# One attention layer's PSUM slots, square buffers and norms rearranged in a two-layer trunk kernel

## The chip, the cores and the metric

The kernel runs on one core of a Trainium2 chip. The metric is the device time of one execution in microseconds, the median of several runs; lower is better. The core has five engines that run their own instruction streams and wait for each other by semaphores: PE (matrix multiplication, with PEld for its weight loads), DVE (vector), ACT (scalar, activations), POOL (the general one) and SP (which issues most transfers here). SBUF is the on-chip memory; PSUM holds what PE writes, and DVE and ACT read it from there.

## The reference

Two layers over x of 512 tokens by 1024 features, all in float32. A layer is: half a SwiGLU feed-forward, a mixer, a cross attention to 256 memory tokens, and another half feed-forward. Layer 0's mixer is a stick-breaking attention with a gated mixing branch; layer 1's is the multi-head latent attention that the change touches:

```
def _mla_mixer(h, positions, w_in, q_lora_g, kv_lora_g, w_uq, w_ukv, q_g, k_g, w_out):
    c_q, c_kv, k_r = jnp.split(h @ w_in, [512, 768], axis=-1)
    q  = (_rmsnorm(c_q, q_lora_g) @ w_uq).reshape(b, s, 16, 96)
    kv = (_rmsnorm(c_kv, kv_lora_g) @ w_ukv).reshape(b, s, 16, 128)
    k_nope, v = kv[..., :64], kv[..., 64:]
    k = concatenate([k_nope, broadcast(k_r to 16 heads)])       # 64 + 32
    q = _rmsnorm(q, q_g);  k = _rmsnorm(k, k_g)                 # over each head's 96
    q, k = (_rope on the last 32 of each)
    o = _causal_softmax_attention(q, k, v)                      # 16 heads, scale 96**-0.5
    return o.reshape(b, s, 1024) @ w_out
```

## The kernel before

x stays in SBUF transposed, as eight tiles of 128 features by 512 tokens. Every large product is split into a high and a low part in a format that PE multiplies faster, and runs as three matmuls (`mm3`, L103 to L105: high by high, low by high, high by low). `split` makes the two parts: a high one (L79, on ACT here) and the rest (L83, on DVE).

`mla_attn` treats the 16 heads in four groups of G = 4. `proj_q(g, t)` makes a block of 128 tokens of the queries of a group (12 matmuls into an "A" bank); ACT copies it out (L716) and squares it into a scratch tile (L718, `dg` with a single buffer), and DVE sums the squares (L719). `proj_kv(g, t)` does the same for keys and values (6 matmuls; square L692, sum L693). The last block of a group (t = 3) ends with `norms` (a chain of small DVE instructions, L666 and L111 to L119), the factors `sqr` (L698), and `knorm`, which multiplies the keys by their inverse norms into `ks`: the 64 features of each head (L673) and the 32 shared ones (L674), for the whole group at once, on DVE for group 0 and on POOL otherwise. Then POOL multiplies the group's `qs` by `sqr` (L700).

The attention is one loop over n = 0 to 16. In step n stand, in the order in which PE runs them:

1. `scores(n)`: three "lg" banks; DVE takes row maxima (L827), ACT exponentials with their sums (L831).
2. `weights` of head n - 1: PE turns the exponentials (L845) into "pt" banks, in three units. ACT copies unit 0 out to wT (L850), DVE units 1 and 2 (L852). Units 0 and 1, then fillers, then unit 2.
3. If n is even and two heads are complete: `inverse`. DVE takes reciprocals of the sums of both heads (L859 to L862), PE turns them (L864) into a "pt" bank, and DVE copies them to arT (L867).
4. `turn` for head n + 2: PE turns q (L740, four transposes into a "pt" bank), then k (another "pt" bank). From q's, ACT makes qTh (L79) and DVE qTl (L83); from k's, ACT makes kTh (L747) and DVE kTl (L748).
5. Fillers.
6. If n is even: `spread` (L872, four matmuls with the selector `asel` into the bank in which the inverse was turned; ACT copies it to rbc, L875) and `values` (L887, 16 matmuls of the two heads into "av"; DVE multiplies by rbc, L894, and the product is split into hh and hl, the input of the output projection).
7. Fillers.

The fillers are the projections of later groups, and behind them the first half of the output projection, taken by `take` in the numbers of the table `FILL`; the first 14 steps (`LEAD2`) stand ahead of the loop. PSUM has in this part two "pt" slots, three "lg", one "av" and two "A". A tile of a pool takes the slot that its name frees next, and the first instruction that writes it waits for the last reader of the tile that had the slot before. PE's instructions run in the order written here.

Of the kernel before, what the change touches and what calls it, by code (L numbers as in the profile page):

```python
# [11 lines left out]
ALU = mybir.AluOpType  # L12
AX = mybir.AxisListType

P = 128
D = 1024
S = 512
KT = D // P
NT = S // P
# [7 lines left out]
class Trunk:  # L27
# [626 lines left out]
    def mla_attn(self, p, pl, pp, cT, krr, skr, gqk, neg, tq, o):  # L654
        nc, a = self.nc, self.a
        G = 4
        LEAD2 = 14
        FILL = [(0, 1, 1)] + [(1, 0, 1)] * 8 + [(2, 0, 2)] * 8
# [10 lines left out]

        def knorm(st, y, eng):  # L670
            st["ks"] = ks = self.t(p, [P, NT, G, 96], "ks", bufs=2)
            by = lambda d: y[:, :, :, None].to_broadcast([P, NT, G, d])
            eng.tensor_tensor(out=ks[:, :, :, 0:64], in0=st["kn"], in1=by(64), op=ALU.mult)  # L673
            eng.tensor_tensor(out=ks[:, :, :, 64:96], in0=krr[:, :, None, :].to_broadcast([P, NT, G, 32]), in1=by(32),  # L674
                              op=ALU.mult)

        def proj_kv(st, g, t):

            if t == 0:
                st["wkv"] = self.gran(a["mla_w_ukv"][g], 2, 512, lo="dve" if g < 2 else "pool")  # L680
                st["v"] = self.t(p, [P, NT, G, 64], "vs", bufs=3)
                st["kn"] = self.t(p, [P, NT, G, 64], "kn", bufs=1)
            cs = slice(t * P, (t + 1) * P)
            ps = self.psA()
            wh, wl = st["wkv"]
            for k in range(2):
                self.mm3(ps, (cT[4 + k][0][:, cs], cT[4 + k][1][:, cs]), (wh[:, k, :], wl[:, k, :]), k == 0, k == 1)
            z = ps.rearrange("p (g d) -> p g d", g=G)
            nc.scalar.copy(out=st["kn"][:, t], in_=z[:, :, 0:64])
            nc.scalar.copy(out=st["v"][:, t], in_=z[:, :, 64:128])  # L690
            s2 = self.t(self.sp, [P, NT, P], "dg", bufs=1)[:, :, 0:64]
            nc.scalar.activation(out=s2, in_=z[:, :, 0:64], func=AF.Square)  # L692
            nc.vector.tensor_reduce(out=st["ss"][:, 0, t, :], in_=s2, axis=AX.X, op=ALU.add)  # L693
            if t < NT - 1:
                return
            y = norms(st)
            st["s"] = self.t(p, [P, NT, G], "sqr", bufs=3)
            ts(out=st["s"], in0=y[:, 1], scalar1=96 ** -0.5, scalar2=None, op0=ALU.mult)  # L698
            knorm(st, y[:, 0], nc.vector if g == 0 else nc.gpsimd)
            nc.gpsimd.tensor_tensor(out=st["qs"], in0=st["qs"], in1=st["s"][:, :, :, None].to_broadcast([P, NT, G, 96]),  # L700
                                    op=ALU.mult)

        def proj_q(st, g, t):

            if t == 0:
                st["wq"] = [self.gran(a["mla_w_uq"][2 * g + i], 2, 384, lo="dve" if g < 2 else "pool") for i in range(2)]
                st["qs"] = self.t(p, [P, NT, G, 96], "qs", bufs=2)
                st["ss"] = self.t(p, [P, 2, NT, G], "ssqk", bufs=2)
            cs = slice(t * P, (t + 1) * P)
            qs = st["qs"]  # L710
            ps = self.psA()
            for k in range(4):
                wh, wl = st["wq"][k // 2]
                self.mm3(ps[:, 0:384], (cT[k][0][:, cs], cT[k][1][:, cs]), (wh[:, k % 2, :], wl[:, k % 2, :]),
                         k == 0, k == 3)
            nc.scalar.copy(out=qs[:, t].rearrange("p g d -> p (g d)"), in_=ps[:, 0:384])  # L716
            s1 = self.t(self.sp, [P, NT, P], "dg", bufs=1)[:, :, 0:96]
            nc.scalar.activation(out=s1, in_=ps[:, 0:384].rearrange("p (g d) -> p g d", g=G), func=AF.Square)  # L718
            nc.vector.tensor_reduce(out=st["ss"][:, 1, t, :], in_=s1, axis=AX.X, op=ALU.add)  # L719
            if t < NT - 1:  # L720
                return

            bc = lambda z: z[:, :, None, :].to_broadcast([P, NT, G, 16])
            q1, q2 = qs[:, :, :, 64:80], qs[:, :, :, 80:96]
            w = [self.t(p, [P, NT, G, 16], f"qr{i}", bufs=1) for i in range(3)]
            rt = nc.gpsimd.tensor_tensor
            rt(out=w[0], in0=q1, in1=bc(tq["c1"]), op=ALU.mult)
            rt(out=w[1], in0=q1, in1=bc(tq["s1"]), op=ALU.mult)
            rt(out=w[2], in0=q2, in1=bc(tq["s2"]), op=ALU.mult)
            rt(out=q1, in0=w[0], in1=w[2], op=ALU.subtract)  # L730
            rt(out=w[2], in0=q2, in1=bc(tq["c2"]), op=ALU.mult)
            rt(out=q2, in0=w[1], in1=w[2], op=ALU.add)
# [60 lines left out]
        def take(n, queue=True):  # L793
            for _ in range(n):
                if queue:
                    with self.queued():
                        next(fill, None)
                else:
                    next(fill, None)
# [55 lines left out]
        def inverse(sm):  # L855


            rc = self.t(p, [P, 2 * NT], "arc", bufs=2)
            nc.vector.reciprocal(out=rc, in_=sm.rearrange("p i t -> p (i t)"))  # L859
            r2 = self.t(p, [P, 2, 2 * NT], "ar2", F32R, bufs=2)  # L860
            nc.vector.tensor_copy(out=r2[:, 0], in_=rc)
            tt(out=r2[:, 1], in0=rc, in1=r2[:, 0].bitcast(F32), op=ALU.subtract)  # L862
            ps = self.t(pp, [P, S], "pt", bufs=2)
            nc.tensor.transpose(out=ps[0:16, 0:P], in_=r2.rearrange("p e r -> p (e r)").bitcast(F32),  # L864
                                identity=self.ident)
            rT = self.t(p, [16, P], "arT", F32R, bufs=2)
            nc.vector.tensor_copy(out=rT, in_=ps[0:16, 0:P])  # L867
            rb = self.rbc

            def spread():  # L870
                for t in range(NT):
                    self.pe = nc.tensor.matmul(ps[:, t * P:(t + 1) * P], lhsT=sel[:, t], rhs=rT, start=(t == 0),  # L872
                                               stop=(t == NT - 1), skip_group_check=True)

                nc.scalar.copy(out=rb, in_=ps)  # L875
                return rb
            return spread

        def values(n, wTs, rb):

            g, h = divmod(n, G)
            av = self.t(pp, [P, S], "av", bufs=1)
            for j in range(NT):
                u, c0 = KA[j]
                wd = S - j * P
                for i, wT in enumerate(wTs):
                    self.pe = nc.tensor.matmul(av[i * 64:i * 64 + 64, j * P:], lhsT=gs[g]["v"][:, j, h + i, :],  # L887
                                               rhs=wT[u][:, c0:c0 + wd], start=(j == 0), stop=(j == NT - 1),
                                               skip_group_check=True)
            f = n // 2  # L890
            hi = self.t(self.hp, [P, S], f"hh{f}", F32R)
            lo = self.t(self.hp, [P, S], f"hl{f}", F32R)
            w = self.t(self.sp, [P, S], "sq", bufs=2)
            tt(out=w, in0=av, in1=rb, op=ALU.mult)  # L894
            self.split(hi, lo, w, "act", "dve")
            o.append((hi, lo))

        take(LEAD2, False)
        def ahead(n):

            assert "s" in gs[n // G]
            with self.queued():
                return turn(gs[n // G], n % G)
# [4 lines left out]
        for n in range(17):  # L908
            old = pb
            if n % 2 == 0 and n:  # L910
                sums = self.sums
            if n < 16:
                with self.queued():
                    pb = scores(n, qk.pop(0))
            if old is not None:
                wT = []
                with self.queued():
                    weights(old, wT, (0, 1))
                take(FILL[n][0])
                with self.queued():  # L920
                    weights(old, wT, (2,))
                wTs.append(wT)
            if len(wTs) == 2:
                with self.queued():
                    spread = inverse(sums)
            if n < 14:
                qk.append(ahead(n + 2))
            take(FILL[n][1])
            if len(wTs) == 2:
                with self.queued():  # L930
                    rb = spread()
                with self.queued():
                    values(n - 2, wTs, rb)
                wTs = []
            take(FILL[n][2])


    def xmem(self, l):
# [267 lines left out]
```

## Time and profile before

| what | value |
|---|---|
| median of 3 runs | 2297.13 us |
| range of the runs | 2290.03 to 2308.14 us |
| the profiled execution's own time | 2289.97 us |
| its span, first to last instruction | 2288.3 us |
| its mean granted PE clock | 0.997 |
| busy: PE, PEld, DVE, ACT, POOL | 98%, 82%, 40%, 38%, 45% |
| DMA | 208.68 MB, 91 GB/s on average |

All durations come from the profiled execution. In a row of the timeline the first number is the start in us from the span's start, the second the duration, and the bracket the idle time of the engine ahead of it with the instruction that ended it. In the groups "busy, mean ns" are followed by the group's idle time and what ended most of it. Matmuls are pipelined and their ends are modelled, so two of them in a row may overlap.

### The profile page before, as it was taken

How to read it: one execution, taken by the hardware profiler on the slowest of the kernel's cores; microseconds unless marked ns; L12 is line 12 of the kernel's file. 1: busy time of each engine (PE TensorE's matmuls, PEld its weight loads, DVE VectorE, ACT ScalarE, POOL GpSimd, SP SyncE). 2: the span in 40 equal slices, each digit the busy share in tenths (PEclk: the TensorE clock that was granted, in tenths of full speed). 3: DMA queues.
4: the chain of work that ended last, by engine and by line, in shares of the span. 5: the costliest groups of instructions: out<-in, count | busy, mean ns of one | idle time of the engine just before them, and what ended most of it. 6: DMA issues, size and time to landing. Idle time of an engine off the chain costs nothing. (4 is left out here: it accounts for less than half of the span.)

```text
span 2288.3 us, 29129 instructions
## 1 busy us (share of the span) xinstructions
PE 2250.2 (98%) x11240; PEld 1885.1 (82%) x11240; DVE 907.2 (40%) x1686; ACT 867.4 (38%) x1443; POOL 1018.3 (45%) x824
## 2 busy tenths in 40 slices
PE   8999999999999999999999999998889999999999
PEld 6888888977988888888888888897668988888887
DVE  5211323466745422123422022376558555221220
ACT  4222333366544332223322232356546544322221
POOL 5545546212243454554554554635322424545543
PEclk9999999999999999999999999999999999999999
DMA  4323324211421332332332332321003412323222
GB/s 157 96 83 111 98 80 128 88 56 57 144 97 63 92 99 82 114 94 82 111 95 83 110 100 79 105 83 51 28 29 111 134 61 83 101 77 117 93 82 93
DMA packets 67354, 208.68 MB, mean 91 GB/s; under 512 B 8592, under 2 KB 10640, under 8 KB 67216
## 3 DMA queue, kind: packets, MB, share of 16 engines
q1 hardware_dynamic: 67216, 206.83, 29.3%
q8 instruction: 88, 1.44, 0.3%
q14 instruction: 50, 0.41, 0.1%
HBM read 204.70 MB, written 2.10 MB: 90 GB/s over the span
## 5 line engine op out<-in xcount | busy, mean ns | idle before, releaser
L97 POOL TENSOR_TENSOR wl<-wr,wh 128x512 fp32r<-128x512 f32 (+2 forms) x752 | 945.9, 1279 | 1083.2 <-ACT wh L92 1083.1
L92 ACT CAST wh<-wr 128x1024 fp32r<-128x1024 f32 (+3 forms) x423 | 408.0, 965 | 1040.2 <-PE mm L104 578.8
L103 PE MATMUL mm<-hh,wh 128*128 128x512 f32 x1424 | 556.6, 391 | 6.8 <-ACT hh L130 6.8
L104 PE MATMUL mm<-hl,wh 128*128 128x512 f32 x1424 | 555.6, 390 | 0.5 <-DVE hl L131 0.5
L105 PE MATMUL mm<-hh,wl 128*128 128x512 f32 x1424 | 555.5, 390 | 0.0
L103 PEld LDWEIGHTS mm<-hh,wh 128*128 128x128 f32 x1424 | 268.2, 188 | 62.3 <-ACT hh L130 6.8
L104 PEld LDWEIGHTS mm<-hl,wh 128*128 128x128 f32 x1424 | 268.2, 188 | 56.8 <-DVE hl L131 1.0
L105 PEld LDWEIGHTS mm<-hh,wl 128*128 128x128 f32 x1424 | 268.2, 188 | 56.2 <-POOL wl L97 0.3
L103 PE MATMUL A<-ah,wh 128*128 128x512 f32 x704 | 277.4, 394 | 0.0
L105 PE MATMUL A<-ah,wl 128*128 128x512 f32 x704 | 276.0, 392 | 0.0
L104 PE MATMUL A<-al,wh 128*128 128x512 f32 x704 | 273.2, 388 | 0.0
L226 DVE TENSOR_TENSOR t<-mm,rbc 128x512 f32<-128x512 f32 x88 | 60.9, 692 | 394.9 <-PE mm L105 394.9
L259 DVE SCALAR_TENSOR_TENSOR x<-A,x 128x512 f32<-128x512 f32 x64 | 44.3, 692 | 358.0 <-PE A L105 358.0
L105 PEld LDWEIGHTS A<-ah,wl 128*128 128x128 f32 x704 | 132.1, 188 | 31.0
L104 PEld LDWEIGHTS A<-al,wh 128*128 128x128 f32 x704 | 132.2, 188 | 29.6
L103 PEld LDWEIGHTS A<-ah,wh 128*128 128x128 f32 x704 | 132.3, 188 | 26.3
L224 DVE TENSOR_TENSOR t<-mm,rbc 128x512 f32<-128x512 f32 x88 | 60.9, 692 | 195.4 <-PE mm L105 188.5
L83 DVE TENSOR_TENSOR al<-t,ah 128x512 fp32r<-128x512 f32 x88 | 82.9, 942 | 60.4 <-ACT ah L79 60.4
L103 PE MATMUL A<-hh,wh 128*128 128x512 f32 x240 | 96.7, 403 | 0.0
L105 PE MATMUL A<-hh,wl 128*128 128x512 f32 x240 | 94.0, 392 | 0.0
L104 PE MATMUL A<-hl,wh 128*128 128x512 f32 x240 | 93.8, 391 | 0.0
L103 PE MATMUL mm<-wh,hh 128*128 128x256 f32 (+1 forms) x288 | 82.2, 285 | 0.0
(331 smaller groups left out, 3224.2 us busy)
## 6 DMA issues: line engine op xcount, KB each, us to landing
wr<-in_w_gu SPq DMA_DIRECT2D x176, 512.0 KB, 3.6
wr<-in_w_dn SPq DMA_DIRECT2D x64, 384.0 KB, 3.1
wr<-in_w_dn SPq DMA_DIRECT2D x64, 320.0 KB, 2.9
wr<-in_xmem_wkv SPq DMA_DIRECT2D x32, 512.0 KB, 3.3
wr<-in_xmem_wq SPq DMA_DIRECT2D x16, 512.0 KB, 3.3
wr<-in_xmem_wo SPq DMA_DIRECT2D x16, 512.0 KB, 3.2
wr<-in_sbg_w_zv SPq DMA_DIRECT2D x12, 512.0 KB, 3.6
wr<-in_sbg_w_qk SPq DMA_DIRECT2D x8, 512.0 KB, 3.6
```

What stands on the lines that cost most here:

```text
L83: e.tensor_tensor(out=lo, in0=src, in1=hi.bitcast(F32), op=ALU.subtract)
L92: nc.scalar.copy(out=hi, in_=raw)
L97: e.tensor_tensor(out=lo_[:, c], in0=raw[:, c], in1=hi[:, c].bitcast(F32), op=ALU.subtract)
L103: mm(out, lhsT=A[0], rhs=B[0], start=start, stop=False, skip_group_check=True)
L104: mm(out, lhsT=A[0], rhs=B[1], start=False, stop=False, skip_group_check=True)
L105: self.pe = mm(out, lhsT=A[1], rhs=B[0], start=False, stop=stop, skip_group_check=True)
L224: nc.vector.tensor_tensor(out=t1, in0=pg, in1=self.rbc, op=ALU.mult)
L226: nc.vector.tensor_tensor(out=t2, in0=pu, in1=self.rbc, op=ALU.mult)
L259: nc.vector.scalar_tensor_tensor(out=self.x[m], in0=ps, scalar=0.5, in1=self.x[m], op0=ALU.mult, op1=ALU.add)
```

## The change

Three edits in `mla_attn`.

1. The turned inverse sums and their spread go to the outputs' bank ("av", one buffer) and no longer to a "pt" slot. The values are then written to the same bank, after the spread was copied out. The fillers of the step that stood behind the values now stand between the spread and the values, together with those that stood ahead of the spread.
2. The squares of `proj_q` and `proj_kv` go to the scratch name "sq" with two buffers; the product of the values with rbc, which had that name, takes "dg" with one.
3. The norms are applied head by head: for each head of the group two products for k (on DVE for group 0, on POOL otherwise) and one on POOL for q, where there were one each for the whole group.

```
         def knorm(st, y, eng):
             st["ks"] = ks = self.t(p, [P, NT, G, 96], "ks", bufs=2)
-            by = lambda d: y[:, :, :, None].to_broadcast([P, NT, G, d])
-            eng.tensor_tensor(out=ks[:, :, :, 0:64], in0=st["kn"], in1=by(64), op=ALU.mult)
-            eng.tensor_tensor(out=ks[:, :, :, 64:96], in0=krr[:, :, None, :].to_broadcast([P, NT, G, 32]), in1=by(32),
-                              op=ALU.mult)
+            for h in range(G):
+                by = lambda d: y[:, :, h, None].to_broadcast([P, NT, d])
+                eng.tensor_tensor(out=ks[:, :, h, 0:64], in0=st["kn"][:, :, h], in1=by(64), op=ALU.mult)
+                eng.tensor_tensor(out=ks[:, :, h, 64:96], in0=krr, in1=by(32), op=ALU.mult)
+                nc.gpsimd.tensor_tensor(out=st["qs"][:, :, h], in0=st["qs"][:, :, h],
+                                        in1=st["s"][:, :, h, None].to_broadcast([P, NT, 96]), op=ALU.mult)
...
-            s2 = self.t(self.sp, [P, NT, P], "dg", bufs=1)[:, :, 0:64]
+            s2 = self.t(self.sp, [P, S], "sq", bufs=2).rearrange("p (g d) -> p g d", g=G)[:, :, 0:64]
...
             knorm(st, y[:, 0], nc.vector if g == 0 else nc.gpsimd)
-            nc.gpsimd.tensor_tensor(out=st["qs"], in0=st["qs"], in1=st["s"][:, :, :, None].to_broadcast([P, NT, G, 96]),
-                                    op=ALU.mult)
...
-            s1 = self.t(self.sp, [P, NT, P], "dg", bufs=1)[:, :, 0:96]
+            s1 = self.t(self.sp, [P, S], "sq", bufs=2).rearrange("p (g d) -> p g d", g=G)[:, :, 0:96]
...
-            ps = self.t(pp, [P, S], "pt", bufs=2)
+            ps = self.t(pp, [P, S], "av", bufs=1)
             nc.tensor.transpose(out=ps[0:16, 0:P], in_=r2.rearrange("p e r -> p (e r)").bitcast(F32),
...
-            w = self.t(self.sp, [P, S], "sq", bufs=2)
+            w = self.t(self.sp, [P, NT, P], "dg", bufs=1).rearrange("p t c -> p (t c)")
             tt(out=w, in0=av, in1=rb, op=ALU.mult)
...
-            take(FILL[n][1])
             if len(wTs) == 2:
                 with self.queued():
                     rb = spread()
+                take(FILL[n][1] + FILL[n][2])
                 with self.queued():
                     values(n - 2, wTs, rb)
                 wTs = []
-            take(FILL[n][2])
+            else:
+                take(FILL[n][1] + FILL[n][2])
```

Lines of the changed kernel lie one to three higher than before (L740 becomes L741, L864 L865, L887 L888, L719 L720, L693 L696).

PE's order at n = 2, from unit 2 of the weights on (pt and av are the PSUM banks, ar the inverse sums, arT their turned copy). Before:

```order
L845 MATMUL pt_12893<-ident_100,pb_2166_12731 128x128 [waits DVE_49]
L845 MATMUL pt_12893<-ident_100,pb_2164_12720 128x128
L864 MATMUL pt_12903<-ident_100,ar_2210_12900 16x128 [waits Activation_49]
L740 MATMUL pt_12907<-ident_100,qs_12473 96x128 [waits DVE_49,Pool_49]
L740 MATMUL pt_12907<-ident_100,qs_12473 96x128 x3
L740 MATMUL pt_12916<-ident_100,ks_12710 96x128 [waits DVE_49]
L740 MATMUL pt_12916<-ident_100,ks_12710 96x128 x3
L872 MATMUL pt_12903<-arT_12905,asel_12291 128x128 x4
L887 MATMUL av_12930<-wT_2170_12749,vs_12390 64x512
```

Of the change, at the same place up to the spread:

```order
L846 MATMUL pt_12911<-ident_100,pb_2166_12749 128x128 [waits DVE_49]
L846 MATMUL pt_12911<-ident_100,pb_2164_12738 128x128
L865 MATMUL av_12921<-ident_100,ar_2210_12918 16x128
L741 MATMUL pt_12925<-ident_100,qs_12482 96x128 [waits Activation_49,Pool_49]
L741 MATMUL pt_12925<-ident_100,qs_12482 96x128 x3
L741 MATMUL pt_12934<-ident_100,ks_12719 96x128 [waits DVE_49]
L741 MATMUL pt_12934<-ident_100,ks_12719 96x128 x3
L873 MATMUL av_12921<-arT_12923,asel_12291 128x128 [waits DVE_49]
L873 MATMUL av_12921<-arT_12923,asel_12291 128x128 x3
```

The inverse now writes "av" without a wait, q waits for ACT (and POOL, which makes qs) where it waited for DVE, and the spread waits for DVE's arT. Twelve filler matmuls follow in the changed kernel, and then the values, whose first now waits for ACT:

```order
L103 MATMUL A_12948<-wh_12785,ch_1999_11773 128x384
L104 MATMUL A_12948<-wl_12786,ch_1999_11773 128x384
L105 MATMUL A_12948<-wh_12785,cl_2000_11774 128x384
L888 MATMUL av_12974<-wT_2170_12767,vs_12390 64x512 [waits Activation_49]
L888 MATMUL av_12974<-wT_2202_12885,vs_12390 64x512
```

The fillers stand ahead of the values, and not behind them.

DVE's order where the norms of group 2 are made, n = 4 to 5, up to the copy of unit 1 (rs_y, rs_u and rs_v belong to the norms' chain, anm to the maxima, dg to the values). Before:

```order
L827 TENSOR_REDUCE anm_13213<-lg_13214 128x1 [waits PE_49]
L666 TENSOR_TENSOR ssqk_12773<-ssqk_12773,skr_11780 128x16 [waits DVE_49]
L111 TENSOR_SCALAR rs_v_13193<-ssqk_12773 128x32 [waits DVE_49]
L827 TENSOR_REDUCE anm_13213<-lg_13222 128x1 [waits PE_49]
L113 TENSOR_SCALAR rs_y_13195<-rs_v_13193 128x32 [waits DVE_49]
L827 TENSOR_REDUCE anm_13213<-lg_13222 128x1
L117 TENSOR_TENSOR rs_u_13197<-rs_y_13195 128x32 [waits DVE_49]
L827 TENSOR_REDUCE anm_13213<-lg_13235 128x1 [waits PE_49]
L118 SCALAR_TENSOR_TENSOR rs_u_13197<-rs_u_13197,rs_v_13193 128x32 [waits DVE_49]
L852 COPY wT_2303_13255<-pt_13250 128x512 [waits PE_49]
```

Of the change, the last twelve rows up to the same copy; right ahead of them stands the product of the values (L895):

```order
L117 TENSOR_TENSOR rs_u_13200<-rs_y_13198 128x32 [waits DVE_49]
L828 TENSOR_REDUCE anm_13240<-lg_13241 128x1 [waits PE_49]
L118 SCALAR_TENSOR_TENSOR rs_u_13200<-rs_u_13200,rs_v_13196 128x32 [waits DVE_49]
L83 TENSOR_TENSOR hl_2291_13235<-dg_13236,hh_2290_13234 128x512 [waits Activation_49]
L119 SCALAR_TENSOR_TENSOR rs_y_13198<-rs_u_13200,rs_y_13198 128x32 [waits DVE_49]
L828 TENSOR_REDUCE anm_13240<-lg_13249 128x1 [waits PE_49]
L117 TENSOR_TENSOR rs_u_13200<-rs_y_13198 128x32 [waits DVE_49]
L828 TENSOR_REDUCE anm_13240<-lg_13249 128x1
L118 SCALAR_TENSOR_TENSOR rs_u_13200<-rs_u_13200,rs_v_13196 128x32 [waits DVE_49]
L828 TENSOR_REDUCE anm_13240<-lg_13262 128x1 [waits PE_49]
L119 SCALAR_TENSOR_TENSOR rs_y_13198<-rs_u_13200,rs_y_13198 128x32 [waits DVE_49]
L853 COPY wT_2303_13282<-pt_13277 128x512 [waits PE_49]
```

The chain begins before the values' product and all of it is ahead of the copy, and the product and hl stand there too.

DVE's order behind the norms' factors of group 0. Before:

```order
L698 TENSOR_SCALAR sqr_12455<-rs_y_12443 128x16 [waits DVE_49]
L673 TENSOR_TENSOR ks_12457<-kn_12391,rs_y_12443 128x16x64
L674 TENSOR_TENSOR ks_12457<-krr_11779,rs_y_12443 128x16x32
L719 TENSOR_REDUCE ssqk_12474<-dg_12506 128x4 [waits Activation_49]
```

Of the change, the last three of the eight and the sum:

```order
L676 TENSOR_TENSOR ks_12457<-krr_11779,rs_y_12443 128x4x32
L675 TENSOR_TENSOR ks_12457<-kn_12391,rs_y_12443 128x4x64
L676 TENSOR_TENSOR ks_12457<-krr_11779,rs_y_12443 128x4x32
L720 TENSOR_REDUCE ssqk_12483<-sq_12515 128x4 [waits Activation_49]
```

Eight products stand ahead of the next sum of squares where there were two.

## The prediction

> **What bounds the kernel now.** I read the page's busy times first, then its forty slices, then stretches of the place that the slices point to, then TensorE's (PE's) waits there, then single instructions.
>
> ```profile
> span 2288.3 us, 29129 instructions
> PE 2250.2 (98%) x11240; PEld 1885.1 (82%) x11240; DVE 907.2 (40%) x1686; ACT 867.4 (38%) x1443; POOL 1018.3 (45%) x824
> PE   8999999999999999999999999998889999999999
> ```
>
> The matmul engine is busy 98% of the span, so only what shortens or stretches PE's own sequence moves the end. Slices 28 to 30, about 57 us each, are the one soft place. They are layer 1's attention, which is where every edit lies.
>
> ```profile
> 1540.00:1560.00 20.00, 15.63 (x87) 13.71 (x86) 14.01 (x27) 11.64 (x27) 13.16 (x13) 1.00 0.15 49
> 1640.00:1700.00 60.00, 52.75 (x293) 38.13 (x292) 34.20 (x74) 28.18 (x73) 13.42 (x10) 0.91 0.09 30
> 1700.00:1740.00 40.00, 39.58 (x226) 31.31 (x225) 25.09 (x48) 20.80 (x49) 9.71 (x8) 1.00 0.18 55
> ```
>
> In each row PE's busy time comes first after the length, then PEld, DVE, ACT, POOL, the granted clock, the DMA share and GB/s. PE idles 4.4 us in the first stretch and 7.2 in the second, and the second alone has a granted clock under 1. DMA is at 9 to 18%: no transfer bounds this part. By the waits and groups of 1540 to 1740 us:
>
> ```profile
> PE A L103 <- ACT dg L718: 3.0, 1, 3.0
> PE pt L864 <- ACT wT L850: 0.7, 1, 0.7
> PE pt L845 <- DVE wT L852: 2.1, 2, 1.4
> L740 PE MATMUL pt<-ident,ks 128*96 128x128 f32 x64 | 10.2, 282 | 10.4 <-DVE qTl L83 8.4 <-DVE wT L852 2.0
> L740 PE MATMUL pt<-ident,qs 128*96 128x128 f32 x64 | 10.0, 279 | 4.0 <-DVE wT L852 1.6 <-DVE qTl L83 1.3 <-ACT wT L850 1.0
> ```
>
> The turns of k wait 8.4 us for qTl, which is the last reader of the turned q. That is a wait for a PSUM slot, since k's transposes read nothing of q. The other rows are a stall for a square (3.0) and smaller waits for copies out of the same "pt" slots. These 21 us are all that the change can win at full clock. Where they stand in a step, here head 2, when the sums of heads 0 and 1 are inverted:
>
> ```profile
> 1579.79 0.27 PE L864 MATMUL pt<-ident,ar 128*16 128x128 f32 x1
> 1580.56 0.61 PE L740 MATMUL pt<-ident,qs 128*96 128x128 f32 x4 [0.50 <-DVE wT L852]
> 1582.57 0.64 PE L740 MATMUL pt<-ident,ks 128*96 128x128 f32 x4 [1.39 <-DVE qTl L83]
> 1583.14 0.66 PE L872 MATMUL pt<-arT,asel 16*128 16x128 f32 x4
> 1583.73 2.38 PE L887 MATMUL av<-wT,vs 128*64 128x512 f32 x16
> 1579.99 0.42 DVE L852 COPY wT<-pt 128x256 f32<-128x256 f32 x1 [1.65 <-PE pt L845]
> 1581.83 0.69 DVE L83 TENSOR_TENSOR qTl<-pt,qTh 96x512 fp32r<-96x512 f32 x1 [0.60 <-ACT qTh L79]
> 1581.21 0.58 ACT L79 CAST qTh<-pt 96x512 fp32r<-96x512 f32 x1 [0.57 <-PE pt L740]
> 1583.25 0.68 ACT L747 ACTIVATE kTh<-pt,gqk 96x512 fp32r<-96x512 f32 x1 [1.46 <-PE pt L740]
> 1583.84 0.58 ACT L875 COPY rbc<-pt 128x512 f32<-128x512 f32 x1
> 1578.72 0.59 ACT L850 COPY wT<-pt 128x512 f32<-128x512 f32 x1
> ```
>
> "pt" has two slots. The inverse takes one at 1579.79 and keeps it until the rbc copy ends at 1584.42. So q must have the slot of weights unit 2, copied by DVE until 1580.41, and k must have q's own, free only at 1582.52 when qTl ends. k starts 0.05 us later.
>
> **Edit 1: the inverse in the outputs' bank.** The inverse no longer holds a slot. In the new order q waits for ACT (unit 0's copy, which ended at 1579.31 here, before PE gets there) and k for unit 2's copy by DVE (1580.41) instead of for qTl (1582.52). The "av" bank was read last two heads earlier, so the inverse finds it free. This takes away 8.4 + 1.6 = 10.0 us at the six pair steps with a turn (n = 2 to 12), and the 0.7 of the inverse on unit 0's slot. Not touched: the 1.3 of q, which is the first turn of all before any inverse. What is late next is unit 2's copy. That is how the odd steps already run, with k waiting for wT (2.0 in the group row) and q for ACT's copy (1.0), 3.0 us over seven odd steps or 0.4 each. With DVE's 0.42 us copy starting 0.2 after the inverse and q's four transposes in between I take 0.33 a step, 2.0 in all, from the bounds 0 and 6 x 0.7. Term: −10.7 + 2.0 = **−8.7** (−10.7 to −6.5).
>
> The price is that spread and outputs now share a bank, so the first matmul of the values (L887) waits for ACT's rbc copy. Behind it on PE stand the other 15, then the next head's scores, for which DVE and ACT wait. The cover is the fill that now stands between: 12 matmuls of a q projection at about 0.17 us between starts, 2.1 us, or six of a kv projection, or six of the output projection. ACT needs qTh 0.58, kTh 0.68 and rbc 0.58, about 1.9 us after q's turn ends; PE meanwhile has k's turn 0.57, the spread 0.59 and the fill, at least 2.5. With 0.6 us of slack I cost it at 0. Without cover it would be up to 1.3 us at each of eight pairs.
>
> **The half clock.** The 0.91 above comes from three short stretches, of which the first and the last stand here (PE's busy time, the clock, the DMA share, GB/s). The first row is a window elsewhere, for the rivals:
>
> ```profile
> 1547.68:1551.10 3.42, 1.77 (x11) 1.00 0.00 0
> 1646.67:1650.08 3.41, 2.02 (x15) 1.00 0.00 0
> 1650.08:1653.49 3.41, 3.41 (x17) 0.50 0.00 0
> 1694.45:1697.87 3.42, 3.42 (x12) 0.50 0.00 0
> 1649.49 4.00 PE L887 MATMUL av<-wT,vs 128*64 128x512 f32 x16
> ```
>
> Each half-clock stretch follows a 3.41 us window that holds a whole k wait (n = 8, 10, 12; PE busy 2.02, 2.02 and 1.79 us of 3.41). At n = 2, 4 and 6 a boundary of the same grid splits the wait, and the clock stays at 1.00. The values take 4.00 us instead of 2.38: 1.6 us lost, three times. With the k waits gone the windows hold under 1 us of idle, and the loss goes: **−4.8** (−5.1, three whole windows at half speed, to 0).
>
> The Trainium skill ("TensorE: Matmul & The Clock Gate", Part 1: The HAM clock gate) puts the return to half rate after at least one idle window of about 3.4 us. The window's length agrees with 3.41 us here; but no window here was idle throughout, and 2.02 us of work did not keep the clock up. [...]
>
> **Edit 2: two buffers for the squares.** The stall of 3.0 us stands in the first group:
>
> ```profile
> 1552.46 0.50 PE L103 MATMUL A<-wh,ch 128*128 128x512 f32 x1 [3.02 <-ACT dg L718]
> 1551.92 0.49 ACT L718 ACTIVATE dg<-A 128x384 f32<-128x384 f32 x1 [4.07 <-DVE ssqk L719]
> 1547.04 1.22 DVE L673 TENSOR_TENSOR ks<-kn,rs_y 128x1024 f32<-128x1024 f32 x1
> 1548.18 3.24 DVE L674 TENSOR_TENSOR ks<-krr,rs_y 128x512 f32<-128x512 f32 x1
> 1551.35 0.54 DVE L719 TENSOR_REDUCE ssqk<-dg 128x4 f32<-128x384 f32 x1
> 1547.28 3.60 POOL L700 TENSOR_TENSOR qs<-qs,sqr 128x1536 f32<-128x1536 f32 x1 [2.54 <-DVE sqr L698]
> ```
>
> PE needs a free "A" bank, ACT's square frees it but needs the single "dg", DVE's sum frees that but stands behind L674, and L674 stands until POOL's 3.60 us end at 1550.88, although by size it is half of L673's 1.22. The second buffer lets one more square pass. It gives one step of 12 matmuls (2.1 us) of room at most, since the square after it needs the same late sum.
>
> **Edit 3: norms head by head.** DVE's sum now stands behind eight norms instead of two, with four POOL products among them:
>
> ```profile
> L700 POOL TENSOR_TENSOR qs<-qs,sqr 128x1536 f32<-128x1536 f32 x4 | 11.9, 2968 | 2.5 <-DVE sqr L698 2.5
> L673 POOL TENSOR_TENSOR ks<-kn,rs_y 128x1024 f32<-128x1024 f32 x3 | 5.7, 1907 | 9.9 <-DVE rs_y L119 9.9
> L674 POOL TENSOR_TENSOR ks<-krr,rs_y 128x512 f32<-128x512 f32 x3 | 3.2, 1051 | 0.0
> ```
>
> From 1051 ns for 512 elements and 1907 for 1024, POOL costs about 0.2 us an instruction and 1.67 ns an element. A head's q product (384) is then about 0.84, and a group's three instructions (5.9 us) become twelve of about 7.6. POOL waits 9.9 us for DVE here and no PE wait is on it, and the first head's k and q are ready after about 2 us instead of 5.9; in groups 1 to 3 I cost this at 0. In group 0 DVE's eight norms sum to about 2.5 us if they run free (1.22 and 0.6 plus six fixed parts of 0.1) and to about 5.5 if they alternate with POOL's four. Today they take 4.3 (1547.04 to 1551.42). The two ends for the stall are gone (−3.0) and longer (+0.3: 1.2 more on DVE, 2.1 of room less 1.2 of what PE can't use). I take **−0.7**, near the far end, because the row of L674 shows the alternation.
>
> The Trainium skill ("SBUF — State Buffer", Who interferes with whom) says that a DVE instruction with two SBUF inputs contends with a GpSimd instruction that reads SBUF, and that the later one blocks wholly. L674's 3.24 us agree. By it the eight small norms could each stand behind a POOL product, and the sum would have +0.3 for this term.
>
> **Where the fills moved.** The step n = 4 (and n = 8) now takes the last kv projection of a group ahead of the values, not behind:
>
> ```profile
> 1610.48 1.15 DVE L111 TENSOR_SCALAR rs_v<-ssqk 128x32 f32<-128x32 f32 x1
> 1613.53 0.68 DVE L852 COPY wT<-pt 128x512 f32<-128x512 f32 x1
> 1614.26 0.44 PE L845 MATMUL pt<-ident,pb 128*128 128x128 f32 x2 [0.69 <-DVE wT L852]
> 1759.93 1.05 PE L152 MATMUL at<-ones,sqs 128*128 128x1 f32 x8 [1.35 <-DVE sqs L145]
> ```
>
> With it DVE's chain of norms starts earlier. But in the new order seven more of its small instructions (0.17 to 0.19 each, about 1.4 us), the product of the values (0.69) and hl (0.69) stand ahead of unit 1's copy: 2.8 us more DVE work, against about 2.3 us of values put in between on PE. The two waits that exist (0.69 and 1.4, the 2.1 row above) grow by about 1.0 each: **+2.0** (−2.0 if the early start wins, +4.0 if the dependent instructions stand as L111 does). At the end, n = 16, the values come after the last fills, so the last head pair's hh and hl, and what the next stage reads of x, come later; the 1.35 us wait of that stage grows: **+1.0** (0 to 2.5).
>
> **Sum**: −8.7 − 4.8 − 0.7 + 2.0 + 1.0 = −11.2 us. Against the profiled execution's 2289.97 us this is 2278.8; against the median of the runs, 2297.13, it is 2285.9. The profiled execution stood at the low end of its runs (2290.03 to 2308.14), so I forecast between: **2282 us**. The bounds of the terms together reach from −21 to +3.
>
> **Rivals.**
> (a) The half clock stays, since something other than the k waits sets it, the skill's rule among the reasons. For it: the window of 1547.68 to 1551.10, which holds most of the 3.0 us stall, was busy for only 1.77 us and the clock stayed whole after it. Against: three of three half windows follow a whole k wait. −11.2 + 4.8 = −6.4, 2287.
> (b) More goes than summed: the stall of group 0 wholly (−2.3 more), no growth at n = 5 and 9 (−2.0), residuals of 0 (−2.0), no later end (−1.0). −11.2 − 7.3 = −18.5: 2271.5 from the profiled execution, 2278.6 from the median.
> (c) The edit only shifts the wait: k stands behind unit 2's copy for 0.7 to 0.9 at each of six steps, because DVE has sums of squares ahead of the copy. −11.2 + 3, and one or two half windows stay: −5, 2288.
> (d) Slower: values behind ACT's rbc copy. It decides where ACT enters the turn more than 0.6 us late at most of eight pairs, through exponentials or a weight cast ahead of qTh. Such a delay holds PE 2 us at eight places, +16, and may halve the clock behind it: 2289.97 + 5, or 2300 by the median. Against: ACT idles 0.57 ahead of qTh and 1.46 ahead of kTh in the rows shown.
>
> **Chances**: forecast 0.55, (a) 0.17, (b) 0.13, (c) 0.08, (d) 0.07. About 1%, 23 us, is what a measurement of this kernel tells from none. Only (b) at its low end, with part of the forecast's tail, passes −23 us: faster 0.14; slower needs (d) at two or three times its price: 0.03; same 0.83. Range 2268 to 2296: at the bottom the whole −21 from the profiled execution, (b), (a) and (c) inside, and at the top (a) and (c) from the median with 4 us of spread; the worse part of (d) is left out.
>
> **What the profile after would show.** Right: no wait of the turn for qTl beyond the first; turns of k waiting for the copy of wT by under 0.5; granted clock 1.00 from 1640 to 1700; PE busy over 56 of 60 us there. Values waiting for rbc would show (d). The group 0 stall at 2 to 3 us, now on a square named "sq", and the waits at n = 5 and 9 of 1.5 to 2.5 us show edits 2, 3 and the fills. Wrong would be the forecast if the even steps keep an idle of over a microsecond under a new name.

## The result and the profile after

The change took the kernel from 2298.38 to 2283.76 us (medians of 12 runs each), a ratio of 0.9937 with a 95% interval of 0.9919 to 0.9954: by the ratio 14.5 us less, 10.6 to 18.6. The profiled execution of after has a span of 2284.0 us, only 4.3 under before's. Most of that gap between the two comparisons lies outside the changed part. The first projection of the attention starts at 1523.73 us before and at 1528.51 after, ahead of any changed line, and from the next stage's sums to the end of the kernel it takes 528.3 us before and 531.4 after. (The last section says what goes with that.) So I compare from landmark to landmark in each trace. They are starts of PE's instructions, but for the end of the last values:

| stretch, us | before | after | difference |
|---|---|---|---|
| first projection to first inverse (n = 2) | 56.06 | 59.07 | +3.01 |
| first to seventh inverse (n = 2 to 14) | 132.37 | 116.32 | −16.05 |
| seventh inverse to the end of the last values | 17.79 | 19.67 | +1.88 |
| end of the last values to the next stage's sums (L152) | 29.98 | 29.02 | −0.96 |
| all | 236.20 | 224.08 | −12.12 |

From the page of after, the span and PE's forty slices:

```profile
span 2284.0 us, 29168 instructions
PE   7999999999999999999999999998999999999999
```

Two stretches of after (columns as in the prediction):

```profile
1558.21:1565.03 6.82, 4.64 (x14) 3.46 (x15) 3.54 (x7) 4.27 (x10) 6.44 (x8) 0.50 0.19 58
1640.00:1700.00 60.00, 57.22 (x355) 44.63 (x354) 41.99 (x94) 35.04 (x91) 17.63 (x22) 1.00 0.11 36
```

The larger of PE's waits of after from 1530 to 1765 us (total, times, longest):

```profile
PE A L103 <- ACT sq L719: 4.2, 1, 4.2
PE pt L741 <- DVE wT L853: 3.9, 6, 1.1
PE at L152 <- DVE sqs L145: 1.8, 1, 1.8
PE pt L741 <- DVE sqr L701: 1.1, 1, 1.1
```

One 8 is left of the three in slices 28 to 30. From 1640 to 1700 us PE is busy 57.2 of 60 us at full clock, where it was 52.8 at 0.91. But the stall of group 0 grew from 3.0 to 4.2 us, and two half-clock windows now stand at it. The timeline of after at the place that the prediction went through, n = 2, PE, then ACT, then DVE:

```profile
1587.58 0.27 PE L865 MATMUL av<-ident,ar 128*16 128x128 f32 x1
1587.69 0.60 PE L741 MATMUL pt<-ident,qs 128*96 128x128 f32 x4
1588.26 0.64 PE L741 MATMUL pt<-ident,ks 128*96 128x128 f32 x4
1588.83 0.66 PE L873 MATMUL av<-arT,asel 16*128 16x128 f32 x4
1591.73 2.38 PE L888 MATMUL av<-wT,vs 128*64 128x512 f32 x16
1589.53 0.58 ACT L876 COPY rbc<-av 128x512 f32<-128x512 f32 x1
1587.78 0.42 DVE L853 COPY wT<-pt 128x256 f32<-128x256 f32 x1 [1.66 <-PE pt L846]
```

No bracket is left on PE: k follows q by 0.57 us where it took 2.01. ACT's copy of the spread ends at 1590.11, 1.6 us before the values want the bank. The timeline of after at group 0's stall, DVE's eight products and the sums that ACT and PE wait for, then POOL:

```profile
1551.81 0.42 DVE L675 TENSOR_TENSOR ks<-kn,rs_y 128x256 f32<-128x256 f32 x1
1552.15 0.93 DVE L676 TENSOR_TENSOR ks<-krr,rs_y 128x128 f32<-128x128 f32 x1
1553.00 1.05 DVE L675 TENSOR_TENSOR ks<-kn,rs_y 128x256 f32<-128x256 f32 x1
...
1557.93 0.82 DVE L676 TENSOR_TENSOR ks<-krr,rs_y 128x128 f32<-128x128 f32 x1
1558.67 1.65 DVE L720 TENSOR_REDUCE ssqk<-sq 128x4 f32<-128x384 f32 x3
1552.05 3.54 POOL L677 TENSOR_TENSOR qs<-qs,sqr 128x384 f32<-128x384 f32 x4 [2.55 <-DVE sqr L701]
1555.55 2.17 POOL L97 TENSOR_TENSOR wl<-wr,wh 128x384 fp32r<-128x384 f32 x2
1557.68 0.91 POOL L728 TENSOR_TENSOR qr<-qs,rt0c 128x256 f32<-128x256 f32 x1
```

The first product takes 0.42 us alone; each later one takes 0.8 to 1.2, while POOL always has an instruction running, first the four products and then the weight splits and the rotation. The eight take 6.9 us where the two took 4.3.

### The profile page after: what moved, and what is told of

The parts are those of the page before. It is cut to its first block, busy times and chain, and to the rows that moved or that the text cites. A ratio compares the mean times of both kernels' runs of the same rounds, so it can differ in the third digit from the quotient of the medians.

```text
span 2284.0 us, 29168 instructions
## 1 busy us (share of the span) xinstructions
PE 2251.1 (99%) x11240; PEld 1888.9 (83%) x11240; DVE 911.5 (40%) x1692; ACT 867.9 (38%) x1443; POOL 1020.1 (45%) x854
```

## The experiments

Each is measured against before on the same chip; the rows come from the profile of the run.

| kernel | median us | ratio to before (95%) | stall of group 0 |
|---|---|---|---|
| edit 1 alone | 2288.83 | 0.9965 (0.9951 to 0.9979) | 3.0 |
| edit 2 alone | 2296.00 | 1.0002 (0.9988 to 1.0016) | 1.6 |
| edit 3 alone | 2297.73 | 1.0011 (0.9995 to 1.0028) | 3.4 |
| full, fillers where they were | 2289.96 | 0.9967 (0.9950 to 0.9984) | 4.1 |
| full, k of group 0 on POOL | 2279.67 | 0.9932 (0.9909 to 0.9954) | none |
| full, group 0 whole | 2279.89 | 0.9928 (0.9907 to 0.9950) | 1.6 |
| before, work put in the waits | 2291.74 | 0.9977 (0.9962 to 0.9992) | 3.0 |
| edit 1, POOL's q product left out | 2284.98 | 0.9944 (0.9929 to 0.9959) | 3.0 |
| edits 1 and 2 | 2284.51 | 0.9943 (0.9922 to 0.9964) | 1.6 |
| full, group 0 split otherwise | 2275.22 | 0.9906 (0.9879 to 0.9934) | none |
| full, again | 2281.61 | 0.9933 (0.9908 to 0.9958) | 4.1 |

**Edit 1 alone.**

```
-            ps = self.t(pp, [P, S], "pt", bufs=2)      # in inverse
+            ps = self.t(pp, [P, S], "av", bufs=1)
...
+                take(FILL[n][1] + FILL[n][2])          # between spread and values
```

> Only edit 1 (inverse and spread in the outputs' bank, fillers ahead of the values). Theory: the slot of the turned inverse carries the whole gain. k's turns wait for qTl only once (the first turn, 1.3 us), the granted clock from 1640 to 1700 us is 1.00, the wait of 2.1 us of unit 1's transposes is gone, the stall of group 0 stays at 3.0 us on dg. Time: 14 us below before (ratio about 0.994), the same as the full change or 1 to 2 us better. Rival: the early first head of edit 3 and the second square buffer carry part of it, then this one gains under 9 us.

The even steps became free of waits but for 1.4 us at n = 10, nearly as expected, but the kernel gained 8 us and not 14. PE's waits in this kernel:

```profile
PE pt L740 <- DVE wT L852: 9.4, 7, 4.8
```

Its timeline at n = 5, PE, DVE and POOL:

```profile
1623.05 1.09 PE L740 MATMUL pt<-ident,ks 128*96 128x128 f32 x4 [4.81 <-DVE wT L852]
1617.46 1.50 DVE L698 TENSOR_SCALAR sqr<-rs_y 128x16 f32<-128x16 f32 x1
1619.99 2.67 DVE L862 TENSOR_TENSOR ar<-arc,ar 128x8 fp32r<-128x8 f32 x1
1619.88 2.75 POOL L700 TENSOR_TENSOR qs<-qs,sqr 128x1536 f32<-128x1536 f32 x1
```

A new wait of 4.8 us stands there (the expectations below call the step n = 4, whose filler starts the norms). An instruction on 8 elements a partition, L862, takes DVE 2.67 us: it ends with POOL's product, 1622.66 and 1622.63. Unit 2's copy is behind it, and k waits for that copy. Two half-clock windows stand there too, from 1619.87 to 1626.69 us. In the timeline of the full change the same instruction takes 0.32 us beside POOL's shorter pieces:

```profile
1620.21 0.32 DVE L863 TENSOR_TENSOR ar<-arc,ar 128x8 fp32r<-128x8 f32 x1
1620.92 0.64 PE L741 MATMUL pt<-ident,ks 128*96 128x128 f32 x4 [1.12 <-DVE wT L853]
```

**Edits 2 and 3 alone.**

```
-  s1 / s2 = self.t(self.sp, [P, NT, P], "dg", bufs=1)...     # edit 2
+  s1 / s2 = self.t(self.sp, [P, S], "sq", bufs=2)...
```

```
+            for h in range(G):                                # edit 3
+                ks[..., h, 0:64], ks[..., h, 64:96], qs[:, :, h]: a product each
```

> Only edit 2 (two buffers for the squares, the values' product in the single one). Theory: the stall of group 0 goes from 3.0 to about 0.9 us, since one step of 12 matmuls (2.1 us) passes before the next square needs the late sum; the k waits of 8.4 us and the half clock stay; time 2 us below before, within the noise. Rival (the stall is set by the A banks alone): it stays at 3.0 us.

> Only edit 3 (norms head by head). Theory: DVE's eight products of group 0 alternate with POOL's instructions and take 6.9 us instead of 4.3, so the stall of 3.0 us on dg grows to about 5.5 us; the k waits stay; time 2 to 6 us above before (2.5 us of stall, up to 3.4 us of half clock behind it). Rival (the products run free on DVE, 2.5 us): the stall shrinks to about 1.2 us and the time falls by 2 us.

Edit 2 shortened the stall to 1.6 us (0.9 expected) and edit 3 lengthened it to 3.4 (5.5 expected): signs right, sizes smaller. Neither moves the time by itself. The k waits for qTl are all there in both, 9.7 and 9.5 us, with four stretches of half clock between 1585 and 1710.

**The fillers back in their places.**

```
+            take(FILL[n][1])
             if len(wTs) == 2: rb = spread(); values(n - 2, wTs, rb)
+            take(FILL[n][2])
```

> The full change, but the fillers stand where they stood before: the values right behind the spread. Theory: without a filler between them the values wait for ACT's rbc copy, 0.6 to 1.3 us at each of the eight pairs (5 to 10 us in all), and the 2.1 us wait of unit 1's transposes at n = 5 and 9 is back: 7 to 12 us above the full change, nearly all of the gain. Rival (ACT is ahead anyway): same time as the full change.

PE's waits in this kernel:

```profile
PE av L888 <- ACT rbc L876: 4.9, 7, 0.7
PE pt L846 <- DVE wT L853: 2.1, 2, 1.4
PE at L152 <- DVE sqs L145: 3.4, 1, 3.4
```

The values now wait for the copy, 0.7 us at most and 4.9 in all, and unit 2's transposes again wait 2.1 us for unit 1's copy (the expectation calls them unit 1's). By the ratios this kernel gains 7.6 us where the full change gains 14.5, and between the landmarks it takes 232.3 us against 224.1: 7 to 8 us lost, at the low end of the 7 to 12 expected. So the cover that the prediction named is real and needed, and rival (d) was a real mechanism that the fillers keep away.

**Work in the waits of before.**

```
+                if nm == "q" and fillq:                       # n = 2 to 12 only
+                    for t in range(5): matmul(av, cT[0][0][:, 0:P], cT[1][0])
```

> The kernel before with five more matmuls of 128x512 (1.2 us of work whose result is never read) between the turns of q and k at n = 2 to 12, where PE waits 1.4 us for qTl. Theory (a window that holds a whole wait sets the half clock): no step gets longer, k's waits fall to 0.2 us, no half-clock window is left between 1570 and 1710 us, and the time falls by 3 to 5 us. Rival (the Trainium skill's rule in TensorE: Matmul & The Clock Gate, Part 1: only a whole idle window does it, so something else makes the three windows): three or four half-clock windows stay and the time is that of before.

Its timeline of PE at n = 2:

```profile
1584.40 0.94 PE L744 MATMUL av<-ch,ch 128*128 128x512 f32 x3
1585.53 0.71 PE L744 MATMUL av<-ch,ch 128*128 128x512 f32 x2
1587.17 0.64 PE L740 MATMUL pt<-ident,ks 128*96 128x128 f32 x4 [0.93 <-DVE qTl L83]
```

The stretch from 1570 to 1710 us, before and in this kernel:

```profile
1570.00:1710.00 140.00, 123.98 (x746) 97.40 (x745) 85.56 (x199) 77.05 (x196) 45.41 (x37) 0.96 0.10 34
1570.00:1710.00 140.00, 128.41 (x797) 103.82 (x795) 88.79 (x206) 80.20 (x207) 47.34 (x39) 1.00 0.10 35
```

Three of the five ran ahead of q, so k still waited 0.93 us; that part of the expectation missed. From one inverse to the next no stretch got longer by more than 0.3 us, and no half-clock window is left between 1570 and 1710 us (before: three, 0.96). The stretches of n = 8 to 13, which held them, are 1.34, 0.94 and 1.36 us shorter. This is not the luck of one trace: over all runs of this kernel the mean granted clock is 0.996 to 0.999, where the runs of before on the same chip have 0.990 to 0.997, and the time falls by 5.3 us (1.8 to 8.7).

So a partly idle window does set the half clock, and rival (a) falls: had something else set it, the windows would have stayed. The other traces agree. Take the windows of 3.41 us between 1530 and 1770 us in all thirteen traces that ran at full clock, 867 of them. Of these, all 22 in which PE was busy for less than 1.75 us were followed by half clock, and of the 67 with 1.75 to 2.4 us of work 14 were; of the others none was. None of the 36 was idle throughout. Transposes count as work in this: a window with 2.10 us of nothing else (edit 1 alone, from 1561.84 us) kept the clock. On this point the trace goes beyond the rule that the Trainium skill ("TensorE: Matmul & The Clock Gate", Part 1: The HAM clock gate) gives in its table of states, which asks for an idle window; here 2.02 us of work in 3.41 was too little. The same part also tells of a kernel in which short idles between groups of matmuls made the clock go back and forth, which is nearer to what stands here.

**Edit 1 without POOL's q product in groups 1 to 3.**

```
+            if g == 0:
                 nc.gpsimd.tensor_tensor(out=st["qs"], in0=st["qs"], ...)
```

> Edit 1 alone, without POOL's product of qs with sqr in groups 1 to 3 (q stays unscaled there, part of the work left out). Theory: in edit 1 alone k waits 4.8 us at n = 4 because DVE's subtraction for the inverse (2.67 us in place of 0.2 to 0.3) stands until POOL's 2.75 us product ends, and unit 2's copy is behind it. Without the product the subtraction takes under 0.9 us and the wait falls to about 2 us. Rival (the wait is for unit 2's copy for another reason): the wait stays above 4 us.

Its timeline at n = 5, DVE and PE:

```profile
1615.35 0.17 DVE L863 TENSOR_TENSOR ar<-arc,ar 128x8 fp32r<-128x8 f32 x1
1615.91 1.09 PE L741 MATMUL pt<-ident,ks 128*96 128x128 f32 x4 [2.30 <-DVE wT L853]
```

2.67 us became 0.17 and the wait 2.30 (about 2 expected). The cause is shown: DVE stood for POOL's long product. The Trainium skill ("SBUF — State Buffer", Who interferes with whom) says that a DVE instruction with two SBUF inputs contends with a GpSimd instruction that reads SBUF. That agrees: L862 has two, and with the product there it took 2.67 us. In the 2.30 us that are left, two DVE instructions with a single input still take 1.50 us (the factors sqr, 16 elements) and 0.86 us (the cast for the inverse, 8 elements), and each ends within 0.03 us of one of POOL's two products of the keys.

**Edits 1 and 2.** The full change without edit 3.

> Edits 1 and 2 without edit 3. Theory: the stall of group 0 is 1.6 us with no half clock behind it, but DVE's inverse stands behind POOL's 2.75 us product at n = 4 and k waits about 4.8 us there, with half clock behind it. Time about 4 us above the variant that has group 0 whole and the other groups head by head, near that of the full change (2283) to 2287. Rival (edit 3 does nothing in groups 1 to 3): 2280.

PE's largest waits for the copies, first in this kernel, then with edit 3 in groups 1 to 3 added (the second of the three kernels that come next):

```profile
PE pt L740 <- DVE wT L852: 9.7, 7, 4.8
PE pt L749 <- DVE wT L861: 4.0, 6, 1.1
```

The wait at n = 5 is there with 4.8 us, and with edit 3 in groups 1 to 3 it is 1.1. From the second to the third inverse the traces have 23.7 us in place of 27.9, and from the first to the seventh 117.8 in place of 124.7. The ratios, 0.9943 and 0.9928, go the same way, though their intervals overlap. In the traces edit 3 does earn about 4 us at n = 4 and 5 and 6.9 us in all in groups 1 to 3, with half clock included (two windows without it, one with it).

**Group 0, three ways.** All of k on POOL head by head; whole as before; whole, with DVE only the 64 features and POOL the 32 shared ones:

```
-            knorm(st, y[:, 0], nc.vector if g == 0 else nc.gpsimd)   # on POOL
+            knorm(st, y[:, 0], nc.gpsimd)
...
+            if eng is nc.vector:                                     # whole: ks 0:64 on DVE, and
+                eng / nc.gpsimd: ks 64:96;  nc.gpsimd: qs            # 64:96 on DVE / split: on POOL
+                return
```

> The full change, with the norms of k of group 0 on POOL too, so DVE has none of the eight products ahead of its sums of squares. Theory (the stall of group 0 is DVE's sum standing behind products that alternate with POOL): the stall of 4.2 us falls under 0.5, the half clock behind it goes (3.4 us lost), the first turn starts 5 to 7 us earlier after the first projection than in the full change (34.0 us there), and the time falls by 4 to 7 us against it. Rival (the A banks or POOL's own chain set it): POOL's twelve instructions, about 7.6 us, hold the first turn of k, and less than 2 us is won.

> The full change, with the norms of group 0 whole as before (two products on DVE, one on POOL), head by head in groups 1 to 3. Theory: the stall is that of edit 2 alone, 1.6 us in place of 4.2, and the short POOL instructions keep what edit 3 wins at n = 4 and 8; 3 to 5 us below the full change. Rival (the early first head of group 0 is needed): the first turn waits for k by over 1 us and the time is that of the full change.

> The full change, with the norms of group 0 in three whole-group products shared out otherwise: DVE only the 64 features of k (1.2 us, started before POOL), POOL the 32 shared ones (1.05 us) and then q (3.0 us). Theory (the stall is DVE's sum behind an instruction that stands until POOL ends): no stall on sq above 0.3 us, POOL is done 4.1 us after sqr and before PE gets to the first turn, no half clock there; from the first projection to the first inverse about 52 us (59.1 in the full change, 54.9 with group 0 as before), so 5 to 8 us below the full change. Rival (POOL's chain now holds the first turn, as with all norms on POOL): 56 us or more.

> The full change again, beside the two others on the same chip: about 14 us below before, a group 0 stall of about 4.2 us with two windows of half clock behind it. If the stall and its windows are a matter of chance, this profile shows another size.

The timeline with all of them on POOL, at the first turns, ACT, DVE and PE:

```profile
1553.20 0.37 ACT L692 COPY kn<-A 128x256 f32<-128x256 f32 x1 [1.57 <-POOL ks L675]
1554.80 0.62 ACT L79 CAST qTh<-pt 96x512 fp32r<-96x512 f32 x1
1555.45 0.69 DVE L83 TENSOR_TENSOR qTl<-pt,qTh 96x512 fp32r<-96x512 f32 x1
1556.29 0.61 PE L741 MATMUL pt<-ident,qs 128*96 128x128 f32 x4 [2.83 <-POOL wl L97]
```

The stall was gone, and a new wait of 2.8 us stood two steps on, with two half-clock windows behind it. The row names POOL's weight split, which merely ends at the same moment. The chain is another: kn has one buffer, POOL reads it until its last key product, ACT's copy for the next group waits 1.57 us for that, qTh is behind that copy, then qTl, and head 1's q needs the slot. From first projection to first inverse it takes 57.4 us, and the ratio of 0.9932 is that of the full change: as the rival had it, little is won. With the whole group as before the stall is 1.6 us and the stretch 54.9; the ratio of 0.9928 is not clear of the full change's, but between the landmarks the trace has 221.1 us against 224.1. The timeline with the split, DVE and POOL:

```profile
1547.46 2.10 DVE L675 TENSOR_TENSOR ks<-kn,rs_y 128x1024 f32<-128x1024 f32 x1
1549.47 1.00 DVE L728 TENSOR_REDUCE ssqk<-sq 128x4 f32<-128x384 f32 x2
1548.43 3.74 POOL L678 TENSOR_TENSOR qs<-qs,sqr 128x1536 f32<-128x1536 f32 x1
```

The stretch of this kernel from 1570 to 1710 us:

```profile
1570.00:1710.00 140.00, 134.01 (x836) 107.93 (x835) 91.67 (x203) 83.61 (x214) 51.66 (x65) 1.00 0.10 35
```

POOL started first after all and the product took 2.10 us where 1.2 was expected, but DVE is at the sum 2.0 us after the product starts, no stall is left, and from first projection to first inverse it takes 53.0 us. This kernel, at 2275.22, lies 22.4 us under before and 6.4 under the full change on the same chip (six runs each, 2274.32 to 2280.76 against 2280.73 to 2286.38). Its ratio is the lowest of the three too, but there the intervals overlap; between the landmarks the traces have 219.2, 221.1 and 222.4 us. The full change, run again, showed the stall of 4.1 us and its two half-clock windows as in its first profile: not chance.

## Why the prediction was right, and where not

The time, 2283.76, lay 1.8 us above the predicted 2282. The sum on the traces came out too: −12.1 us between landmarks against −11.2. The mechanism of the main term was right: k waited for a slot, and with the slot free that wait is gone. That the sum fits so well is in part luck, since terms off by 5.7 and 3.7 us in opposite directions cancel in it. Of the signs that the prediction named, these came as said: no wait for qTl beyond the first turn, a granted clock of 1.00 and over 56 us of PE work from 1640 to 1700 us, and waits of 2.0 and 1.7 us at n = 5 and 9. The stall of group 0 did not (4.2 us, not 2 to 3), nor did k's waits for the copy at n = 1 and 5 (1.1 us, not under 0.5).

- **Edit 1, sized too small.** For edit 1 and the fillers the prediction had −8.7 and +2.0 in the stretch from first to seventh inverse, −6.7 together. The traces give −16.05; less the −3.64 of the half clock (the experiment with work in the waits) that is −12.4, for edit 1, the fillers and edit 3 in groups 1 to 3 together. PE's idle time in that stretch went from 15.15 to 5.36 us, 9.8 less. The term that was mis-sized is the residual: 2.0 us of waiting was to stay at the even steps, because they were to look like the odd ones, and none stayed. At n = 2 DVE was idle for 1.66 us ahead of unit 2's copy and could start it at once. At the odd steps three small instructions for the next inverse stand ahead of it (0.65 us the last of them at n = 3). The remaining 2.6 us (12.4 less 9.8) are not in the waits, and the runs don't say where they come from.
- **Edit 3 in groups 1 to 3, costed at 0.** No PE wait was on POOL there, so I saw nothing to win. With edit 1 in, there is: DVE stands behind a long POOL product, and k behind DVE. The prediction had neither that wait, which edit 1 alone brings, nor its going, which edit 3 brings. In the full change the two omissions cancel; without edit 3 the stretch is 6.9 us longer (124.7 against 117.8).
- **The half clock.** Predicted −4.8, measured −3.6 in the one pair of traces: the mechanism right, the size a third too large there. The prediction took the whole stretch of the slowed values as lost; that this is why is not shown. The medians, 5.3 us (1.8 to 8.7) with work in the waits, do not tell the two sizes apart.
- **Edits 2 and 3 in group 0, wrong in sign.** Predicted −0.7, measured +3.0, with a bound of +0.3. The far bound took DVE's eight products to alternate with POOL's four and then to run free. They ran against the weight splits and rotations queued behind on POOL too, 6.9 us in place of at most 5.5, and the half clock came on top. The +3.0 is the profile of before at its best: in three other traces with the same group 0 (edit 1 alone, work in the waits, edit 1 without the q product) a half-clock window stands at the stall, and the stretch takes 57.2 to 57.5 us instead of 56.1.
- **The fillers' move, +2.0.** PE's waits at n = 5 and 9 were 1.8 and 1.9 us before (0.69 + 0.48 + 0.63, and 1.43 + 0.48) and are 2.0 and 1.7 after (the rows below and k's turn). Before, unit 2's transposes waited for unit 1's copy; now the turn of q does (at n = 9 the row names the instruction right behind that copy). The wait moved and did not grow. The kv projection one slot earlier starts the chain early enough to pay for the work it puts ahead.
- **The end, +1.0.** +1.88 − 0.96 = +0.9, the predicted size. But the wait of the next stage, which was to grow by it, went from 1.35 only to 1.8 us, and in the second trace of the full change to 1.4.

The timeline of after at n = 5 and 9, for the fillers' move:

```profile
1619.16 0.64 PE L741 MATMUL pt<-ident,qs 128*96 128x128 f32 x4 [0.91 <-DVE wT L853]
1659.15 0.44 PE L846 MATMUL pt<-ident,pb 128*128 128x128 f32 x2 [0.43 <-ACT wT L851]
1660.66 0.61 PE L741 MATMUL pt<-ident,qs 128*96 128x128 f32 x4 [1.07 <-DVE sqr L701]
```

Rival (c), k behind unit 2's copy, shows with more than 0.3 us only at n = 1 and 5, 1.1 us each, and not at the even steps; (d) is what the fillers hold off. Two sums of the prediction are off, without effect on the forecast: the waits in its rows add up to 20.2 us and not 21, and the bounds of its terms reach from −20.8 to +0.3, not to +3.

## What to carry to other kernels

A wait for a reader of another tile is a wait for a slot: look for who keeps the other slot, and move that one out. Before lengthening a row of small instructions on one engine, list everything that is queued on the engine it can stand behind, not only its own partners; and look again at an edit that "hides" once another edit has taken its cover. Cost edits together: 2 and 3 measured as nothing alone, and with edit 1 they are 5 to 7 us.

## What the runs showed of the hardware that I had not expected

The profiles of all eleven experiments and of the two kernels split in two by something ahead of every changed line. Where the first half-clock stretch of the kernel begins at 24 to 25 us, the first projection starts at 1523.3 to 1524.2; where it begins at 32 to 33 us, at 1526.8 to 1528.6. The grid of 3.41 us windows thus falls differently on each execution, and 3 to 5 us of scatter come with it before any edit counts. Cause and effect are not separated here. Likewise the same end of the attention was followed by no, one or two half-clock windows (0.0, 1.4 to 1.6 or 3.0 to 3.1 us more to the end of the kernel), whether or not that part differed.

The runs show the same from outside. The 70 runs of before beside the experiments go from 2289.8 us at a mean granted clock of 0.997 to 2307.9 us at 0.990. By an estimate from these two clocks, 0.7% of 2300 us, up to 16 us of these 18 are half clock. With work in the waits the runs spread only from 2288.3 to 2296.3 us. So a good part of the scatter of before goes with the k waits, and its profiled execution, at 0.997, is one of its best: the medians hold more half clock than the pair of profiles, which may be why they differ by 14.5 us and not by 12.1.
